# Delta-rule heads of a hybrid block: SiLU, gate exponentials, corner copies and norm roots set behind the next weights' high part, and both heads' transposes ahead of their copies

## The chip, the cores and the metric

One core of a Trainium2 chip runs the whole program in one launch. The metric is device microseconds (us) of an execution, and the median of several executions counts. The profile is of one such execution.

## The reference, cut to what matters

One encoder layer on 256 tokens with width 2048, all in float32:

```
h    = rms_norm(x, norm_mix_w) * (1 + scale_m) + shift_m
proj = h @ w_in                      # q,k,v,o of the mLSTM; q|k|v, z, beta, decay of the delta rule; two merge gates
qkv  = silu(centred_depthwise_conv(b_qkv, gdn_conv_w))          # 16 heads of 128
q_b  = l2_normalize(q) * B_DK ** -0.5;  k_b = l2_normalize(k)
o_b  = gated_delta_chunkwise(...) forward + backward            # needs the inverse of a unit triangular matrix
o_b  = rms_norm(o_b, gdn_norm_w);  y_b = (o_b * silu(b_z)) @ w_branch_b
h_a  = mLSTM forward + backward;   y_a = (sigmoid(a_o) * rms_norm(h_a)) @ w_branch_a
x    = x + gate_m * ((g_a * y_a + g_b * y_b) @ w_out)
x    = x + gate_f * (silu(gt) * up) @ w_down;   out = rms_norm(x)
```

The shifts, scales and gates come from `silu(c) @ ada_w + ada_b`, a 2048 by 12288 matrix that VectorE multiplies and sums row block by row block (`ada`, L110).

## The kernel before, in words

**Weights in two parts.** Every large projection is computed with each float32 weight split in two: `wh` is the weight rounded to the fast matmul format (a copy on ScalarE), `wl` is the rest (a subtraction on VectorE), and TensorE adds three products: high by high, high by low, low by high. A job loads 1 MB (`raw`, on SyncE's queue, three buffers) and cuts it into two halves. For each half ScalarE writes `wh`, VectorE writes `wl` (three buffers each), and TensorE then runs the half. `fjob` (L132, wh at L141, wl at L142) makes 128 features by 256 tokens, and its halves are named by 0 and 8; `tjob` (L153, wh at L166, wl at L167) makes 512 features for both token halves, with halves 0 and 2 of each of four chunks. So in the order `wh_z_0_2` is the second half of the first chunk of the z projection.

**The delta rule between the weights.** The first projection (L493) makes the gates and the q, k, v of heads 0 to 3. Then come 16 heads in four groups of four. For each head: `gdn_conv` copies a projection into a padded tile (`pad`, L279), applies the five taps (one on ScalarE L281, four on VectorE L283) and SiLU (L284) to give `kq` or `vf`. `gdn_phase1` builds the decays from scans (`dec`, L526 to L529), squares q and k (L534), transposes v and sums the squares on TensorE (`vps`, L537 and L539), takes a root (L546), forms k by k and k by q (`ks`, L565), multiplies by the decays on VectorE (L570 to L580), sends the diagonal blocks out (`inst_d`, L586, on GpSimd's queue) and copies the block corners (`cc`, L594 and L597, six calls on ScalarE).

For each group `gdn_invert` inverts the 32 by 32 diagonal blocks on VectorE (`uu`: a memset at L612, then 30 pairs of L617 and L623). `gdn_blocks` reads the inverses back, mixes them and copies them into `X` (L651) and into the diagonal of `UL` (L656, eight copies a group, all on ScalarE). `gdn_phase2` works on a pair of heads: four small matmul steps `p` (L671, L680, L693, L705) that complete `UL`, the applications `pa` (L718), `pb` (L729), `pc` (L718) and `po` (L744), the norm of each head (`gdn_norm`: squares L765, a root L769, a scaling L774), the transposes `px` (L754) and the copies `obt` (L756), which are stored. Head e's transposes are followed by head e's copy, and then comes the next head. Both heads' transposes write one PSUM tile.

**Fills and streams.** The delta rule is a long chain of small steps, so halves of the large projections stand between them: `fill(n)` issues n halves of jobs waiting in a list (z, v, o, the mLSTM's q and k called `a`, the merge gates `ma` and `mb`), and `stream` issues those of the next heads' q, k, v (`b`). The counts at each step are written out by hand (`after`, `last`, `fill(4)` in `invert`, `drive(..., 3)`). The sums of `ada` are pumped in every second job or so. What stands between two fills is placed by the program's order, with a scheduler that moves some instructions on each engine unless `order(...)` keeps them. On its engine each instruction waits for all ahead of it.

**After the delta rule** the scratch memory is closed (`sx.close`), and SyncE loads the stored heads (`o`, L877) and the mLSTM's q and k, v, and output gates (`mkq` L886, `vt` L888, `sgo` L890), while the last a and ma halves run. Then come the mLSTM, the branch projections, the output projection and the feed-forward part, none of which the diff touches.

A function in ScalarE's table (SiLU, the exponential, the root, the sigmoid) needs the table loaded: the profile shows `ACT_TABLE_LOAD` at the line of the function that follows.

Of the kernel before, what the change touches and what calls it, by code (L numbers as in the profile page):

```python
# [12 lines left out]
ALU = mybir.AluOpType  # L13
# [39 lines left out]
def hybrid_block(ctx: ExitStack, tc: tile.TileContext, xr, nfr, crow, pk_d, cst_d, ada2, ada4, win0, winb, wint, wba, wbb, wo, wgu, wd, out, dbg=None):  # L53
# [61 lines left out]

    background = []
# [15 lines left out]
    def fjob(name, src, done):  # L132
# [5 lines left out]
        for k0 in range(0, KB, 8):  # L138
            wh = st.tile([P, 8, P], F32R, tag="wh", bufs=3, name=f"wh_{name}_{k0}")
            wl = st.tile([P, 8, P], F32R, tag="wl", bufs=3, name=f"wl_{name}_{k0}")  # L140
            S.activation(wh, raw[:, k0 : k0 + 8], AF.Copy)  # L141
            V.tensor_tensor(wl, raw[:, k0 : k0 + 8], wh.bitcast(F32), ALU.subtract)  # L142
            for k in range(8):
                kk = k0 + k
                PE.matmul(o, wh[:, k], hh[:, kk], start=kk == 0, stop=False)  # L145
                PE.matmul(o, wh[:, k], hl[:, kk], start=False, stop=False)  # L146
                PE.matmul(o, wl[:, k], hh[:, kk], start=False, stop=kk == KB - 1)  # L147
            if k0:
                pump()
                done(o)  # L150
            yield True

    def tjob(name, chunks, xh, xl, done, early=0, by_token=False, steps=1):  # L153
# [6 lines left out]
        def halves(u, k0):  # L160
# [5 lines left out]
            order(S.activation(wh, raws[u][:, k0 : k0 + 2], AF.Copy), early)  # L166
            order(V.tensor_tensor(wl, raws[u][:, k0 : k0 + 2], wh.bitcast(F32), ALU.subtract), early)  # L167
# [96 lines left out]
    def gdn_conv(h, j, ps):  # L264
# [19 lines left out]
        S.activation(kq[:, j] if j < 2 else vf, cv, AF.Silu)  # L284
        if ps is None:
            evict(3 * h + j + 1 + NP_)
# [54 lines left out]
    def gates(w0, zz, first):  # L341
# [38 lines left out]
        S.activation(s2[32:64], sp[32:64], AF.Exp)  # L380
        G.dma_start(alpha_d.rearrange("d h t -> (d h) t"), s2[32:64])
# [16 lines left out]
        S.activation(ex[R], ex[R], AF.Exp)  # L398
        for v in range(2):
            r0 = 64 + 4 * v  # L400
            G.dma_start(mal_d[v], ex[r0 : r0 + 4, v, 0])
# [117 lines left out]
    def gdn_phase1(h):  # L519
        if h < GRP:  # L520
# [21 lines left out]
        yield  # L542
        sm = bk.tile([P, 12], F32, tag="sm", bufs=NB + 1, name=f"sm{h}")
# [48 lines left out]
        for b in range(4):  # L592
            r0, c0 = 32 * b, 32 * (b ^ 1)
            S.activation(cc[r0 : r0 + 32, 0, :, c0 : c0 + 32], (mb if b % 2 else mi)[r0 : r0 + 32, 0:2, c0 : c0 + 32], AF.Copy)  # L594
        for b in range(2):
            r0, c0 = 64 * b, 64 * (b ^ 1)
            S.activation(cc[r0 : r0 + 64, 1, :, c0 : c0 + 64], (mb if b else mi)[r0 : r0 + 64, 0:2, c0 : c0 + 64], AF.Copy)  # L597
# [34 lines left out]
    def gdn_blocks(g):  # L632
# [20 lines left out]
        for i, a in enumerate((F_, B_)):  # L653
            for b in range(4):
                r = slice(32 * b, 32 * b + 32)
                order(S.activation(UL[r, i, :, r], a[r], AF.Copy))  # L656
            yield

    def gdn_phase2(g, p):
# [90 lines left out]
        yield  # L750
        for e, on in enumerate(ons):
            h, hl_ = 4 * g + 2 * p + e, 2 * p + e
            for t in range(2):
                PE.transpose(px[:, (2 * e + t) * P : (2 * e + t + 1) * P], on[:, t], ident)  # L754
            obt = bk.tile([P, T], F32, tag="obt", bufs=2, name=f"obt{h}")
# [4 lines left out]
    def gdn_norm(g, h, hl_, po, r4):  # L760
# [8 lines left out]
        S.activation(so[:, 2:4], so[:, 2:4], AF.Sqrt, bias=epsc, scale=1.0 / (DK_B * DK_B))  # L769
        V.reciprocal(so[:, 2:4], so[:, 2:4])  # L770
        V.scalar_tensor_tensor(so[:, 4:6], rq, DK_B**-0.5, so[:, 2:4], ALU.mult, ALU.mult)
        sz = szs[g]
        for t in range(2):
            V.scalar_tensor_tensor(  # L774
                on[:, t], po[:, t * P : (t + 1) * P], so[:, 4 + t : 5 + t], sz[:, t, hl_ * P : (hl_ + 1) * P], ALU.mult, ALU.mult
            )
# [55 lines left out]
    def invert(g):  # L832
        gen = gdn_invert(g)
        next(gen)
        fill(4)
# [4 lines left out]
    for g in range(4):  # L840
# [503 lines left out]
```

## Time and profile before

| what | value |
|---|---|
| median of 3 executions | 2101.28 us (2100.79 to 2106.48) |
| the profiled execution | 2101.75 us |
| its span, first to last instruction | 2100.0 us |
| mean granted TensorE clock | 0.990 |
| TensorE (PE) busy | 2030.5 us, 97% |
| VectorE (DVE) busy | 1397.2 us, 67% |
| ScalarE (ACT) busy | 1056.9 us, 50% |
| GpSimd (POOL) busy | 95.8 us, 5% |

Stages by time from the span's start: first projection 0 to 147 us; gates 147 to 190; the first four heads to 260; the delta rule's groups with their fills to 975; the last fills, the mLSTM and the branch projections to 1250; output projection and norm to 1375; the feed-forward part to 2100.

A row of the timeline gives start, duration, engine, line, operation, output and inputs, and in brackets how long the engine was idle ahead of it and what ended that. The row of a stretch (windows) gives for each engine the busy time and, in parentheses, the number of instructions, then the granted clock as a share of full speed (PEclk), the share of time in which the DMA engines were busy, and GB/s. A group's row ends in its total busy time and the mean of one in ns, then the idle time ahead of it. Queues that issue DMAs are named by a q (SPq is SyncE's).

### The profile page before, as it was taken

Reading aid. Unit: us, or ns where it says so; the run is one execution under the profiler, and the core shown is the slowest. Engines: PE = TensorE matmul, PEld = TensorE weight load, DVE = VectorE, ACT = ScalarE, POOL = GpSimd, SP = SyncE. Lnnn points to the kernel's source line nnn. Section 1 sums busy time; section 2 is a strip of 40 time slices with the busy share of each in tenths; the row PEclk is TensorE's granted clock in tenths of the full one; section 3 lists DMA queues with packets and bytes.
Section 4 is the critical chain, followed back from the end, with each engine's and each line's share of the span. In section 5 each row is a group of like instructions: output and inputs, shape, how many; then the busy total and the mean of one; then the engine's idle time right before and its main releaser. Section 6 shows DMA issues by size and latency. Waiting matters only on the chain.

```text
span 2100.0 us, 27019 instructions
## 1 busy us (share of the span) xinstructions
PE 2030.5 (97%) x10374; PEld 1698.0 (81%) x10374; DVE 1397.2 (67%) x2060; ACT 1056.9 (50%) x1583; POOL 95.8 (5%) x189
## 2 busy tenths in 40 slices
PE   8999999999999999999999999799999999999998
PEld 6777789978988898888777877678888888878886
DVE  6787777777877687754677778665565554455554
ACT  3147548756774666565444443554444444444443
POOL 0002210110111011100000000000000000000000
PEclk9999999999999999999999999999999999999999
DMA  9986664566766565667886778466666665555553
GB/s 401 420 315 190 170 222 154 167 195 236 235 192 208 193 215 212 233 248 264 306 298 229 259 282 311 169 215 238 229 247 233 222 256 183 195 191 194 199 185 137
DMA packets 82035, 485.65 MB, mean 231 GB/s; under 512 B 10585, under 2 KB 20065, under 8 KB 27505
## 3 DMA queue, kind: packets, MB, share of 16 engines
q1 hardware_dynamic: 68736, 459.34, 60.4%
q0 software_dynamic: 5856, 9.49, 3.0%
q10 hardware_dynamic: 7314, 15.10, 1.9%
q8 instruction: 81, 1.33, 0.3%
q14 instruction: 48, 0.39, 0.1%
HBM read 467.07 MB, written 16.82 MB: 230 GB/s over the span
## 4 chain that ended last, share of the span: by engine, by line
PE 70%; DVE 6%; ACT 5%; DMA 5%; issue 2%; SPq 0%; ACTq 0%; DVEq 0%
PE acc_up L188 4%; PE acc_up L189 4%; PE acc_up L190 4%; PE acc_d L188 4%; PE acc_d L190 4%; PE acc_d L189 4%; PE acc_gt L189 4%; PE acc_gt L190 4%; PE acc_gt L188 4%; PE acc_b L147 2%; PE acc_b L145 2%; PE acc_b L146 2%; DMA ada<-ada 2%; PE acc_o L190 2%; PE acc_o L188 2%
## 5 line engine op out<-in xcount | busy, mean ns | idle before, releaser
L167 DVE TENSOR_TENSOR wl_d<-raw_d,wh_d 128x1024 fp32r<-128x1024 f32 x88 | 107.8, 1226 | 119.8 <-ACT wh_d L166 119.8
L167 DVE TENSOR_TENSOR wl_up<-raw_up,wh_up 128x1024 fp32r<-128x1024 f32 x88 | 107.7, 1225 | 110.0 <-ACT wh_up L166 110.0
L167 DVE TENSOR_TENSOR wl_gt<-raw_gt,wh_gt 128x1024 fp32r<-128x1024 f32 x88 | 107.9, 1226 | 100.0 <-ACT wh_gt L166 100.0
L145 PE MATMUL acc_b<-hh,wh_b 128*128 128x256 f32 x576 | 164.0, 285 | 4.2 <-ACT wh_b L141 4.2
L110 DVE SCALAR_TENSOR_TENSOR ada<-ada,crow 128x2048 f32<-128x2048 f32 x64 | 146.4, 2288 | 29.4 <-DMA ada<-ada 29.0
L147 PE MATMUL acc_b<-hh,wl_b 128*128 128x256 f32 x576 | 161.3, 280 | 1.4 <-DVE wl_b L142 1.4
L166 ACT ACTIVATE wh_d<-raw_d 128x1024 fp32r<-128x1024 f32 x88 | 93.3, 1060 | 137.4 <-PE acc_d L189 132.3
L146 PE MATMUL acc_b<-hl,wh_b 128*128 128x256 f32 x576 | 160.3, 279 | 0.0
L166 ACT ACTIVATE wh_gt<-raw_gt 128x1024 fp32r<-128x1024 f32 x88 | 93.3, 1060 | 127.0 <-PE acc_gt L189 77.2
L166 ACT ACTIVATE wh_up<-raw_up 128x1024 fp32r<-128x1024 f32 x88 | 93.2, 1060 | 117.4 <-PE acc_up L189 84.1
L189 PE MATMUL acc_gt<-wh_gt,hfl 128*128 128x512 f32 x352 | 139.1, 395 | 2.4 <-DVE hfl L1160 2.4
L188 PE MATMUL acc_gt<-wh_gt,hfh 128*128 128x512 f32 x352 | 137.9, 395 | 0.0
L190 PE MATMUL acc_gt<-wl_gt,hfh 128*128 128x512 f32 x352 | 137.7, 391 | 0.0
L188 PE MATMUL acc_up<-wh_up,hfh 128*128 128x512 f32 x352 | 137.1, 389 | 0.5 <-ACT wh_up L166 0.5
L189 PE MATMUL acc_up<-wh_up,hfl 128*128 128x512 f32 x352 | 137.0, 389 | 0.0
L190 PE MATMUL acc_up<-wl_up,hfh 128*128 128x512 f32 x352 | 136.9, 389 | 0.0
L188 PE MATMUL acc_d<-wh_d,ffh 128*128 128x512 f32 x344 | 134.4, 391 | 0.0
L189 PE MATMUL acc_d<-wh_d,ffl 128*128 128x512 f32 x344 | 134.4, 391 | 0.0
L190 PE MATMUL acc_d<-wl_d,ffh 128*128 128x512 f32 x344 | 133.9, 389 | 0.0
L493 PE MATMUL first<-x,raw 128*128 128x256 f32 x512 | 114.5, 382 | 7.8 <-ACT x L487 7.2
L493 PEld LDWEIGHTS first<-x,raw 128*128 128x128 f32 x512 | 96.1, 190 | 26.3 <-ACT x L487 13.8
L145 PEld LDWEIGHTS acc_b<-hh,wh_b 128*128 128x128 f32 x576 | 108.9, 189 | 4.6 <-ACT wh_b L141 4.5
(365 smaller groups left out, 5272.9 us busy)
## 6 DMA issues: line engine op xcount, KB each, us to landing
ada<-ada SPq DMA_DIRECT2D x64, 1024.0 KB, 5.1
raw_gt<-wgu SPq DMA_DIRECT2D x44, 1024.0 KB, 5.0
raw_up<-wgu SPq DMA_DIRECT2D x44, 1024.0 KB, 4.9
raw_d<-wd SPq DMA_DIRECT2D x44, 1024.0 KB, 4.8
raw_b<-winb SPq DMA_DIRECT2D x36, 1024.0 KB, 5.1
ra<-ada SPq DMA_DIRECT2D x32, 1025.0 KB, 15.6
raw<-win SPq DMA_DIRECT2D x16, 1024.0 KB, 14.6
raw_z<-wint SPq DMA_DIRECT2D x16, 1024.0 KB, 5.3
```

Of the source, the lines that this page charges most:

```text
L110: V.scalar_tensor_tensor(raw, raw, 1.0, row_c[:, :D], ALU.mult, ALU.mult, accum_out=mod[:, c0 + b : c0 + b + 1])
L145: PE.matmul(o, wh[:, k], hh[:, kk], start=kk == 0, stop=False)
L146: PE.matmul(o, wh[:, k], hl[:, kk], start=False, stop=False)
L147: PE.matmul(o, wl[:, k], hh[:, kk], start=False, stop=kk == KB - 1)
L166: order(S.activation(wh, raws[u][:, k0 : k0 + 2], AF.Copy), early)
L167: order(V.tensor_tensor(wl, raws[u][:, k0 : k0 + 2], wh.bitcast(F32), ALU.subtract), early)
L188: PE.matmul(ps[t], xh[:, kk, c], wh[:, k], start=kk == 0, stop=False)
L189: PE.matmul(ps[t], xl[:, kk, c], wh[:, k], start=False, stop=False)
L190: PE.matmul(ps[t], xh[:, kk, c], wl[:, k], start=False, stop=kk == last)
L493: PE.matmul(first[o], raw[:, o], x[:, b], start=b == 0 and o % 2 == 0, stop=b == KB - 1 and o % 2 == 1)
```

## The change

A list `behind` holds pieces of work that have been written but not yet issued, and `settle()` issues them. It is called in both kinds of jobs right behind `wh` and ahead of `wl`, at the start of `gdn_phase1`, ahead of its root, ahead of `px`, in the next `gdn_conv` (which leaves one piece in the list) and at the end. Into the list go: SiLU of each convolution; the two exponentials of the gates with the DMAs that store them; the corner copies of each head; and, in `gdn_norm`, the root with the scaling behind it. All but the DMAs and the VectorE part of the scaling are then kept in program order.

Three more edits: four of the eight copies of a group into the diagonal of `UL` (those with i = 1) go to VectorE; `px` of both heads is issued ahead of both `obt`; and the first group's inversion starts with six halves instead of four.

```
+    behind = []
+    def settle(keep=0):
+        while len(behind) > keep:
+            behind.pop(0)()
...
             S.activation(wh, raw[:, k0 : k0 + 8], AF.Copy)
+            settle()
             V.tensor_tensor(wl, raw[:, k0 : k0 + 8], wh.bitcast(F32), ALU.subtract)
...
             order(S.activation(wh, raws[u][:, k0 : k0 + 2], AF.Copy), early)
+            settle()
...
+        settle(1)
         cv = fr.tile([P, T], F32, tag="cv", bufs=2, name=f"cv{h}_{j}")
...
-        S.activation(kq[:, j] if j < 2 else vf, cv, AF.Silu)
-        if ps is None:
-            evict(3 * h + j + 1 + NP_)
+        def end():
+            order(S.activation(kq[:, j] if j < 2 else vf, cv, AF.Silu))
+            if ps is None:
+                evict(3 * h + j + 1 + NP_)
+        behind.append(end)
...
-        S.activation(s2[32:64], sp[32:64], AF.Exp)
-        G.dma_start(alpha_d.rearrange("d h t -> (d h) t"), s2[32:64])
+        def factors():
+            order(S.activation(s2[32:64], sp[32:64], AF.Exp))
+            G.dma_start(alpha_d.rearrange("d h t -> (d h) t"), s2[32:64])
+        behind.append(factors)
...
     def gdn_phase1(h):
+        settle()
...
         yield
+        settle()
         sm = bk.tile([P, 12], F32, tag="sm", bufs=NB + 1, name=f"sm{h}")
...
-            S.activation(cc[r0 : r0 + 32, 0, :, c0 : c0 + 32], (mb if b % 2 else mi)[r0 : r0 + 32, 0:2, c0 : c0 + 32], AF.Copy)
...
+        def corners():
+            for b in range(4):
+                r0, c0 = 32 * b, 32 * (b ^ 1)
+                order(S.activation(cc[r0 : r0 + 32, 0, :, c0 : c0 + 32], (mb if b % 2 else mi)[r0 : r0 + 32, 0:2, c0 : c0 + 32], AF.Copy))
...
+        behind.append(corners)
...
-                order(S.activation(UL[r, i, :, r], a[r], AF.Copy))
+                if i:
+                    order(V.tensor_copy(UL[r, i, :, r], a[r]))
+                else:
+                    order(S.activation(UL[r, i, :, r], a[r], AF.Copy))
...
         yield
+        settle()
         for e, on in enumerate(ons):
             h, hl_ = 4 * g + 2 * p + e, 2 * p + e
             for t in range(2):
                 PE.transpose(px[:, (2 * e + t) * P : (2 * e + t + 1) * P], on[:, t], ident)
+        for e in range(2):
+            h, hl_ = 4 * g + 2 * p + e, 2 * p + e
             obt = bk.tile([P, T], F32, tag="obt", bufs=2, name=f"obt{h}")
             S.activation(obt, px[:, e * T : (e + 1) * T], AF.Copy, scale=pk[:, PK_GNW + h : PK_GNW + h + 1])
...
-        S.activation(so[:, 2:4], so[:, 2:4], AF.Sqrt, bias=epsc, scale=1.0 / (DK_B * DK_B))
...
+        def scaled():
+            order(S.activation(so[:, 2:4], so[:, 2:4], AF.Sqrt, bias=epsc, scale=1.0 / (DK_B * DK_B)))
+            V.reciprocal(so[:, 2:4], so[:, 2:4])
+            V.scalar_tensor_tensor(so[:, 4:6], rq, DK_B**-0.5, so[:, 2:4], ALU.mult, ALU.mult)
...
+        behind.append(scaled)
...
     def invert(g):
         gen = gdn_invert(g)
         next(gen)
-        fill(4)
+        fill(4 if g else 6)
```

In the whole program ScalarE has 60 table loads instead of 70, and 16 copies fewer; VectorE has 16 more. TensorE's instructions are the same in number.

**ScalarE at the end of the second group's second pair** (620 us in the trace; `so` are the norm roots, `nn` the root of the last head's squares, `cc` its corners, `ev` evictions of a projection, `obt` the copies of `px`). Before:

```order
L296 ACTIVATE ev_o_5396<-acc_o_1_4022 128x512
L546 ACT_TABLE_LOAD
L546 ACTIVATE nn_5480<-vps_5407,epsc 128x4
L556 ACTIVATE vv_5486<-vps_5407,nn_5480 128x128
L594 ACTIVATE cc_1107<-mi_5489 32x2x32 x2
L594 ACTIVATE cc_1107<-mb_5490 32x2x32 x2
L597 ACTIVATE cc_1107<-mi_5489 64x2x64
L597 ACTIVATE cc_1107<-mb_5490 64x2x64
L756 ACTIVATE obt_5521<-px_1_5327,pk 128x256
L166 ACTIVATE wh_z_0_0_5534<-raw_z_0_5532 128x1024
L757 DMA ob_d_115<-obt_5521 128x256
L756 ACTIVATE obt_5526<-px_1_5327,pk 128x256
```

And now:

```order
L806 ACT_TABLE_LOAD
L806 ACTIVATE so_5378<-so_5378,epsc 128x2
L806 ACTIVATE so_5384<-so_5384,epsc 128x2
L148 ACTIVATE wh_a_1_8_5510<-raw_a_1_5480 128x1024
L174 ACTIVATE wh_z_0_0_5596<-raw_z_0_5594 128x1024
L317 ACTIVATE ev_a_0_5462<-acc_a_0_5389 128x256
L570 ACTIVATE nn_5542<-vps_5472,epsc 128x4
L174 ACTIVATE wh_z_0_2_5612<-raw_z_0_5594 128x1024
L174 ACTIVATE wh_z_1_0_5630<-raw_z_1_5628 128x1024
L790 ACTIVATE obt_5585<-px_1_5364,pk 128x256
L790 ACTIVATE obt_5588<-px_1_5364,pk 128x256
L620 ACTIVATE cc_1107<-mi_5551 32x2x32
```

The two roots share a table load with each other and with `nn`; three halves' `wh` stand ahead of the copies, and the corners behind them. The weights of z no longer stand behind a copy that waits for a transpose.

**VectorE at the first inversion** (252 to 262 us; `uu` is the inverse in work, `dec` a decay scan of a later head). Before:

```order
L167 TENSOR_TENSOR wl_v_0_2_1700<-raw_v_0_1681,wh_v_0_2_1699 128x1024
L527 SCALAR_TENSOR_TENSOR dec_2471<-al_2215,cst 128x128
L528 SCALAR_TENSOR_TENSOR dec_2471<-al_2215,cst 128x256
L529 SCALAR_TENSOR_TENSOR dec_2471<-al_2215,cst 128x128
L167 TENSOR_TENSOR wl_v_1_0_1727<-raw_v_1_1724,wh_v_1_0_1726 128x1024
L612 MEMSET uu_1234 64x32
L617 TENSOR_TENSOR utmp_1640<-uu_1234 64x30
```

And now:

```order
L176 TENSOR_TENSOR wl_v_0_2_1700<-raw_v_0_1681,wh_v_0_2_1699 128x1024
L552 SCALAR_TENSOR_TENSOR dec_2505<-al_2249,cst 128x128
L176 TENSOR_TENSOR wl_v_1_0_1718<-raw_v_1_1715,wh_v_1_0_1717 128x1024
L176 TENSOR_TENSOR wl_v_1_2_1734<-raw_v_1_1715,wh_v_1_2_1733 128x1024
L640 MEMSET uu_1234 64x32
L645 TENSOR_TENSOR utmp_1640<-uu_1234 64x30
```

The memset stands one low part later.

**SyncE at the end of the delta rule** (975 to 995 us; the merge gate's chunks `raw_ma` around the loads of the mLSTM). Before:

```order
L163 DMA raw_ma_0_9095<-wint 128x2048
L877 DMA o_0_8885<-ob_d_114 128x4x256
L877 DMA o_1_8887<-ob_d_115 128x4x256
L886 DMA mkq_8951<-kq_d_94 128x4x256
L888 DMA vt_8953<-v_d_98 128x1024
L890 DMA sgo_8955<-o_d_102 128x1024
L886 DMA mkq_8960<-kq_d_95 128x4x256
L888 DMA vt_8962<-v_d_99 128x1024
L890 DMA sgo_8964<-o_d_103 128x1024
L877 DMA o_2_9131<-ob_d_116 128x4x256
L163 DMA raw_ma_1_9133<-wint 128x2048
L163 DMA raw_ma_2_9199<-wint 128x2048
```

And now:

```order
L171 DMA raw_ma_0_9092<-wint 128x2048
L171 DMA raw_ma_1_9126<-wint 128x2048
L916 DMA o_0_8944<-ob_d_114 128x4x256
L916 DMA o_1_8946<-ob_d_115 128x4x256
L925 DMA mkq_9010<-kq_d_94 128x4x256
L927 DMA vt_9012<-v_d_98 128x1024
L929 DMA sgo_9014<-o_d_102 128x1024
L925 DMA mkq_9019<-kq_d_95 128x4x256
L927 DMA vt_9021<-v_d_99 128x1024
L929 DMA sgo_9023<-o_d_103 128x1024
L171 DMA raw_ma_2_9164<-wint 128x2048
L916 DMA o_2_9162<-ob_d_116 128x4x256
```

With two halves more issued at the first inversion, all later fills stand two halves earlier: one chunk more is loaded ahead of the block of loads, and `raw_ma_2` stands ahead of `o_2`.

More of the change, by code (lines that the diff above doesn't have):

```diff
@@ L397, in gates, with weights @@
             yield
[L398 to L401, printed above, removed]
+        def weights():
+            order(S.activation(ex[R], ex[R], AF.Exp))
+            for v in range(2):
+                r0 = 64 + 4 * v
+                G.dma_start(mal_d[v], ex[r0 : r0 + 4, v, 0])
+        behind.append(weights)
         gdn_conv(1, 0, None)
@@ L591, in gdn_phase1 @@
         cc = ccs[h % NB]
-        for b in range(4):
-            r0, c0 = 32 * b, 32 * (b ^ 1)
-            S.activation(cc[r0 : r0 + 32, 0, :, c0 : c0 + 32], (mb if b % 2 else mi)[r0 : r0 + 32, 0:2, c0 : c0 + 32], AF.Copy)
-        for b in range(2):
-            r0, c0 = 64 * b, 64 * (b ^ 1)
-            S.activation(cc[r0 : r0 + 64, 1, :, c0 : c0 + 64], (mb if b else mi)[r0 : r0 + 64, 0:2, c0 : c0 + 64], AF.Copy)
+        def corners():
+            for b in range(4):
+                r0, c0 = 32 * b, 32 * (b ^ 1)
+                order(S.activation(cc[r0 : r0 + 32, 0, :, c0 : c0 + 32], (mb if b % 2 else mi)[r0 : r0 + 32, 0:2, c0 : c0 + 32], AF.Copy))
+            for b in range(2):
+                r0, c0 = 64 * b, 64 * (b ^ 1)
+                order(S.activation(cc[r0 : r0 + 64, 1, :, c0 : c0 + 64], (mb if b else mi)[r0 : r0 + 64, 0:2, c0 : c0 + 64], AF.Copy))
+        behind.append(corners)
         heads[h] = (cc, gg, at, vv, r4, sg3)
@@ L768, in gdn_norm @@
         V.tensor_tensor(so[:, 2:4], so[:, 2:4], so[:, 0:2], ALU.mult)
-        S.activation(so[:, 2:4], so[:, 2:4], AF.Sqrt, bias=epsc, scale=1.0 / (DK_B * DK_B))
-        V.reciprocal(so[:, 2:4], so[:, 2:4])
-        V.scalar_tensor_tensor(so[:, 4:6], rq, DK_B**-0.5, so[:, 2:4], ALU.mult, ALU.mult)
         sz = szs[g]
[L773 to L776, printed above, removed]
+        def scaled():
+            order(S.activation(so[:, 2:4], so[:, 2:4], AF.Sqrt, bias=epsc, scale=1.0 / (DK_B * DK_B)))
+            V.reciprocal(so[:, 2:4], so[:, 2:4])
+            V.scalar_tensor_tensor(so[:, 4:6], rq, DK_B**-0.5, so[:, 2:4], ALU.mult, ALU.mult)
+            for t in range(2):
+                V.scalar_tensor_tensor(
+                    on[:, t], po[:, t * P : (t + 1) * P], so[:, 4 + t : 5 + t], sz[:, t, hl_ * P : (hl_ + 1) * P], ALU.mult, ALU.mult
+                )
+        behind.append(scaled)
         return on
@@ L865, in hybrid_block @@
             invert(g + 1)
+    settle()
     sx.close()
```

## The prediction

> **What bounds the kernel now.** I read the page first, then the stages in windows, then each of TensorE's waits in the timeline, and last the granted clock around them.
>
> ```profile
> PE 2030.5 (97%) x10374; PEld 1698.0 (81%) x10374; DVE 1397.2 (67%) x2060; ACT 1056.9 (50%) x1583; POOL 95.8 (5%) x189
> PE 70%; DVE 6%; ACT 5%; DMA 5%; issue 2%; SPq 0%; ACTq 0%; DVEq 0%
> ```
>
> TensorE bounds it: busy 97% of the span and 70% of the chain that ended last. The change takes nothing from TensorE's work, so it can only win the time in which TensorE stands still, and the time in which it runs at a lower clock. The windows show where that is, in the stages that the diff touches:
>
> ```profile
> 147.00:190.00 43.00, 37.97 (x167) 29.54 (x165) 36.07 (x64) 29.62 (x41) 7.27 (x14) 1.00 0.67 202
> 190.00:260.00 70.00, 66.94 (x280) 52.00 (x280) 48.21 (x116) 41.40 (x77) 16.20 (x30) 0.95 0.61 179
> 480.00:617.00 137.00, 135.67 (x991) 124.16 (x990) 108.13 (x203) 102.64 (x198) 14.27 (x28) 1.00 0.70 234
> 617.00:720.00 103.00, 92.39 (x550) 81.97 (x551) 72.52 (x130) 56.28 (x89) 9.92 (x19) 0.95 0.55 186
> 975.00:1000.00 25.00, 24.96 (x179) 23.02 (x178) 9.53 (x8) 9.21 (x12) 2.17 (x4) 1.00 0.93 317
> ```
>
> The second number less the third is TensorE's idle time: 5.0 us in the gates, 3.1 and 10.6 at 190 and 617, but only 1.3 in the long stretch from 480. So the delta rule is mostly covered already, and the loss sits in a few places. These are TensorE's waits there, in order of time; the bracket has the idle time and what ended it:
>
> ```profile
> 161.25 0.51 PE L188 MATMUL acc_z<-wh_z,hh 128*128 128x512 f32 x1 [1.51 <-ACT wh_z L166]
> 163.63 0.74 PE L190 MATMUL acc_z<-wl_z,hh 128*128 128x512 f32 x2 [0.46 <-DVE wl_z L167]
> 172.65 0.50 PE L190 MATMUL acc_v<-wl_v,hh 128*128 128x512 f32 x1 [1.64 <-DVE wl_v L167]
> 220.12 0.44 PE L537 MATMUL vps<-cst,vf 128*128 128x128 f32 x2 [1.02 <-ACT vf L284]
> 221.70 0.80 PE L190 MATMUL acc_v<-wl_v,hh 128*128 128x512 f32 x1 [1.14 <-DVE wl_v L167]
> 260.88 0.50 PE L190 MATMUL acc_v<-wl_v,hh 128*128 128x512 f32 x1 [1.77 <-DVE wl_v L167]
> 515.62 0.38 PE L718 MATMUL pa<-vv,UL 128*128 128x128 f32 x1 [1.12 <-ACT UL L656]
> 620.89 0.69 PE L754 MATMUL px<-cst,on 128*128 128x128 f32 x2 [3.95 <-ACT obt L756]
> 621.84 0.79 PE L188 MATMUL acc_z<-wh_z,hh 128*128 128x512 f32 x1 [0.26 <-ACT wh_z L166]
> 702.42 0.42 PE L145 MATMUL acc_b<-hh,wh_b 128*128 128x256 f32 x1 [1.94 <-ACT wh_b L141]
> 716.99 0.38 PE L145 MATMUL acc_b<-hh,wh_b 128*128 128x256 f32 x1 [2.26 <-ACT wh_b L141]
> 718.25 0.38 PE L147 MATMUL acc_b<-hh,wl_b 128*128 128x256 f32 x1 [0.76 <-DVE wl_b L142]
> 1003.82 0.80 PE L188 MATMUL acc_ma<-wh_ma,hh 128*128 128x512 f32 x1 [3.83 <-ACT wh_ma L166]
> ```
>
> Most are ended by a weight part that ScalarE or VectorE made late. The granted clock shows a second price:
>
> ```profile
> 221.30:228.13 6.83, 6.43 (x19) 5.46 (x20) 3.72 (x12) 3.20 (x8) 0.56 (x1) 0.50 0.79 133
> 262.30:265.71 3.41, 3.41 (x9) 2.69 (x9) 3.24 (x8) 1.06 (x1) 0.00 (x0) 0.50 0.65 269
> 620.70:627.53 6.83, 6.38 (x15) 4.74 (x16) 4.63 (x6) 3.94 (x6) 3.02 (x7) 0.50 0.66 95
> 702.60:706.01 3.41, 3.41 (x17) 3.41 (x18) 1.45 (x2) 2.77 (x6) 0.00 (x0) 0.50 0.35 98
> 1003.00:1009.83 6.83, 6.01 (x14) 4.75 (x15) 6.03 (x10) 4.52 (x5) 0.42 (x1) 0.50 0.62 219
> ```
>
> Each stretch has half the clock. The work done in it would have taken half its busy time, so the drops cost 6.43/2 = 3.2, 1.7, 3.2, 1.7 and 3.0 us. Their starts lie on a grid: 41.0, 358.4, 81.9 and 300.4 us apart are 12, 105, 24 and 88 times 3.413. And in the cell of 3.41 us ahead of each start TensorE was idle for 1.02 + 0.74, 1.77, 3.75, 1.94 and 3.0 us, while the wait of 1.64 us ahead of 172.65 lies inside one cell (170.1 to 173.5 on this grid) and was followed by none, and that of 2.26 us ahead of 716.99 is cut at 716.25 into 1.52 and 0.74. So as I read it a cell that is idle for more than about 1.7 us, half of it, halves the next one or two. A wait under 1.7 us costs itself; a longer one costs 1.7 to 3.2 us more, if its place in the cell is bad.
>
> [...]
>
> **The change part by part.**
>
> *Gates (147 to 190).* What ScalarE does ahead of the late high part at 161 us:
>
> ```profile
> 157.30 0.42 ACT L284 ACTIVATE kq<-cv 128x256 f32<-128x256 f32 x1 [3.96 <-DVE cv L283]
> 158.41 1.28 ACT L380 ACT_TABLE_LOAD   x1
> 160.14 1.06 ACT L166 ACTIVATE wh_z<-raw_z 128x1024 fp32r<-128x1024 f32 x1
> ```
>
> ScalarE waits 3.96 us for taps, then does SiLU, a table load and the exponential, and only then `wh`. In the new order that `wh` stands behind the padding copy and ahead of the next taps and the exponential: the waits of 1.51 and 0.46 go (1.97). Behind the exponential are queued its own store, the decay loads and their scans, which now stand behind a low part that they stood ahead of; for the 1.64 I take half, 0.8. Ends: 0 and 5.0, the stage's whole idle time. Taken: 2.8.
>
> *First inversion (260).*
>
> ```profile
> 258.76 0.20 DVE L617 TENSOR_TENSOR utmp<-uu 64x30 f32<-64x30 f32 x1 [5.28 <-issue]
> ```
> ```profile
> 261.38 0.23 PE acc_v L188
> ```
>
> The first row is VectorE's: it stands 5.28 us at the memset of `uu` until the blocks have come back by DMA, and the low parts behind it stand too. The second, of the chain, is one of TensorE's steps there at the full clock. The new order has one more low part ahead of the memset, which is one half more of TensorE's work, 12 such steps or 2.75 us; that covers the 1.77 us with 1.0 to spare, and the drop of 1.7 goes with it. Taken: 3.5. Ends: 0 and 3.5.
>
> *Diagonal of UL (515).* Four copies leave ScalarE's queue ahead of `pa` and join VectorE's, between taps:
>
> ```profile
> L656 ACT ACTIVATE UL<-cg 32x256 f32<-32x256 f32 x32 | 13.2, 412 | 0.3
> L707 DVE COPY UL<-p 64x256 f32<-64x256 f32 x8 | 3.4, 428 | 1.7 <-ACT UL L706 1.5
> ```
>
> No row shows these copies on VectorE; the nearest, its copy at L707, has 428 ns against ScalarE's 412, and reads PSUM, not SBUF. Four would take 1.7 us on either engine, so `pa` waits about as long as before: I take 0.4 gained, between 1.12 and a loss of 1.7 in each of four groups.
>
> *Transposes and roots (620).* ScalarE's copy that released the second head's transposes started here:
>
> ```profile
> 619.72 0.31 ACT L597 ACTIVATE cc<-mi 64x128 f32<-64x128 f32 x1
> 620.37 0.47 ACT L756 ACTIVATE obt<-px,pk 128x256 f32<-128x256 f32 x1
> L769 ACT ACT_TABLE_LOAD x14 | 18.0, 1283 | 0.2
> ```
>
> The copy is the second row. It stood behind the last root of `vps` and the corners, which waited for VectorE, and z's first `wh` stood behind it. Now the second head's transposes don't need it, and `wh_z_0_0` stands ahead of the last root: 3.95 + 0.26 and the drop of 3.2 go. Next late is `on`, whose root stands ahead of `wh_a_1_8` with one table load for both heads (1.28 us by the third row, where there were two), a whole half of TensorE earlier. Taken: 7.4. Ends: 3.0 and 7.4. What stands behind the copies now is the corners, needed only in the next group.
>
> *Streams (700 and 715).*
>
> ```profile
> 714.64 0.42 ACT L284 ACTIVATE kq<-cv 128x256 f32<-128x256 f32 x1 [3.91 <-DVE cv L283]
> ```
>
> At 715 ScalarE stands 3.91 us in front of a SiLU with `wh_b` behind it. That is what the list takes away: of 2.26 + 0.76 I take 2.5. The 1.94 at 702 is a `wh_b` behind the copies of L656 in a row, after a weight that came late; half of the copies stay, so I take half of 1.94 + 1.7, 1.8. Taken: 4.3. Ends: 0 and 6.7.
>
> *Fills two halves earlier (1003).*
>
> ```profile
> 991.74 0.37 SPq L877 DMA_DIRECT2D o<-ob_d  x1
> 992.97 2.17 SPq L163 DMA_DIRECT2D raw_ma<-wint  x3
> 1002.71 1.06 ACT L166 ACTIVATE wh_ma<-raw_ma 128x1024 fp32r<-128x1024 f32 x1 [11.24 <-DMA raw_ma<-wint]
> ```
>
> `raw_ma_1` was issued at 992.97 behind the block of loads and landed 9.7 us later. In the new order it stands ahead of the block, and `raw_ma_2`, the next one behind it, stands ahead of `o_2`: issued 1.2 us sooner, with half a megabyte less in front (1.6 us at the 317 GB/s of the window from 975). But the fills left behind the block are the same in number, so the wait doesn't go: it shrinks from 3.83 to about 1.0, under half a cell, and the drop of 3.0 may go. Between 0 and 6.8 I take 4.0. The loads of `o` now stand behind a `raw` that waits for a buffer, which delays the mLSTM's first loads by at most a half or two; those loads have TensorE's eight halves behind them.
>
> *What is left alone:* the waits ended by `vf` and `wl_v` at 220 (VectorE has the same work there in both orders), those of `wl` between the steps of the later inversions, and all behind 1090.
>
> *Sum.* 2.8 + 3.5 + 0.4 + 7.4 + 4.3 + 4.0 = 22.4 us. Against it stands what the new order will expose: SiLU, roots and corners of 16 heads come a `wh` later, VectorE has 16 copies more, and every weight load moves. The trace has no row for that. From below it is nothing; from above all the 22.4. I take two new waits of the size of that at 260.88 with its drop, 3.5 each: 7.0. That leaves 15.4 us. The profiled execution took 2101.75 us (2100.0 and 1.75 around it) and the median is 2101.28, so the numbers hold for both: 2101.3 - 15.4 = 2086 us.
>
> **The rivals.**
>
> *More than I take.* Nothing new is exposed, and the drop at 221 goes as well, since its cell was idle by only 1.76 us and the grid will lie otherwise: 22.4 + 3.2 = 25.6, so 2076 us. For it: most of the waits ended by weights are of the same kind, and the list acts on all of them. Against: ScalarE and VectorE work in order, and something is always last.
>
> *Given back at pa.* The diagonal's copies on VectorE stand behind taps and a low part, in stretches where VectorE is busy 108.13 of 137 us. If `pa` of each group waits 1.7 us longer and each time loses 1.7 us of clock, that is 4 x 3.4 = 13.6 on top of the 7.0: 1.8 us are left, 2099.5 us, no change. For it: `pa` is already late by 1.12 us at 515. Against: ScalarE has 1.7 us less there and makes the other four sooner.
>
> *Slower: SiLU and roots come late.* This row shows what they would stand behind:
>
> ```profile
> L141 ACT ACTIVATE wh_b<-raw_b 128x1024 fp32r<-128x1024 f32 x72 | 75.3, 1057 | 42.2 <-PE acc_b L146 23.8 <-DMA raw_b<-winb 12.0 <-PE acc_o L189 4.4
> ```
>
> A `wh` takes 1.06 us and often waits, for a weight to land or a buffer that TensorE still reads; a SiLU behind it waits too, and with it `vps`, as a root does with `px`. That is 16 + 8 places at 1.06 + 0.41 = 1.5 us. It decides when over half of them are bare: 12 x 1.5 = 18, with half of those losing about 2.4 us of clock, 14: 32 - 22.4 = 10 us slower, 2111 us. For it: `vps` waited for `vf` at 220. Against: of 16 heads only that one did, and a half of TensorE's work usually lies between.
>
> **How the numbers follow.** My forecast has 0.51, the larger gain 0.20, the gain given back 0.19, slower 0.10. A measurement of this kernel can tell about 0.3%, 6.3 us, from no change: faster is under 2095, and both first cases lie there, 0.71; same 0.19; slower 0.10. The range goes from 2072, a little past the larger gain, to 2101, past the one given back: some 0.05 lies below it and 0.15 above.
>
> **What would show it.** In the new profile the rows of `px` and `acc_z` at 620 should have no wait of over 1 us and no slice at half clock; the stage at 617 should have under 5 us of idle TensorE in 100; the wait on `wl_v` at 260 should be gone; the one on `wh_ma` near 990 should be under 2 us. The drops should be two or three instead of five up to 1010. I am wrong if `vps`, `px` or `pa` show new waits of over 1.5 us in several groups, or if the waits on `wh` and `wl` in the streams are still there, ended by the same lines at other times.

## The result, and the profile after

| kernel | median, us | lowest to highest | executions |
|---|---|---|---|
| before | 2101.34 | 2097.92 to 2107.58 | 8 |
| changed | 2086.05 | 2078.75 to 2095.21 | 8 |

The changed kernel takes 0.9927 of the time of before, 95% interval 0.9909 to 0.9946: 15.3 us faster. The forecast was 2086. As the experiments show, the total came out right, but several of its terms were credited to the wrong edit. Two single executions further down (one of the kernel before, 2542 us, and one with five halves, 5111 us) were in a far slower state and are left out of the ratios and of the medians given here.

The profiled execution is the slowest of the eight: 2095.21 us, of which the span is 2093.4. It is 6.5 us shorter than the profiled one of before, and not 15; what it shows is a place, not the whole gain. In windows of the stages (TensorE's busy time is the second number, the granted clock the third from the end):

```profile
147.00:190.00 43.00, 38.88 (x174) 30.63 (x173) 38.56 (x72) 30.07 (x43) 8.65 (x15) 1.00 0.68 205
190.00:260.00 70.00, 68.60 (x299) 53.18 (x298) 53.94 (x128) 46.71 (x83) 14.90 (x29) 1.00 0.64 192
480.00:617.00 137.00, 135.09 (x1015) 125.40 (x1014) 112.94 (x219) 96.93 (x199) 13.04 (x26) 1.00 0.71 236
617.00:720.00 103.00, 100.81 (x648) 90.14 (x647) 80.58 (x148) 60.45 (x93) 9.66 (x19) 1.00 0.59 199
720.00:960.00 240.00, 231.81 (x1389) 202.33 (x1389) 168.43 (x307) 139.62 (x253) 18.07 (x34) 0.98 0.65 221
```

From 190 to 260 TensorE is now idle 1.4 us (3.1 before) and from 617 to 720 2.2 us (10.6 before), both at the full clock. The gates won only 0.9 us. In the last row 8.2 us are idle (2.1 in the longer stretch of before), and the clock fell too, to a mean of 0.98 (1.00 in that stretch of before). The waits behind these numbers, from TensorE's timeline:

```profile
175.06 0.50 PE L199 MATMUL acc_v<-wl_v,hh 128*128 128x512 f32 x1 [0.74 <-DVE wl_v L176]
179.59 0.50 PE L199 MATMUL acc_v<-wl_v,hh 128*128 128x512 f32 x1 [1.50 <-DVE wl_v L176]
...
219.43 0.44 PE L560 MATMUL vps<-cst,vf 128*128 128x128 f32 x2 [1.09 <-ACT vf L296]
...
514.71 0.49 PE L749 MATMUL pa<-vv,UL 128*128 128x128 f32 x2 [0.67 <-DVE UL L685]
...
747.85 1.46 PE L711 MATMUL p<-R,pt 128*128 128x32 f32 x6 [3.29 <-DVE pt L703]
...
903.62 0.68 PE L760 MATMUL pb<-z,gg 128*128 128x128 f32 x4 [2.29 <-DVE r L761]
...
997.33 0.80 PE L197 MATMUL acc_ma<-wh_ma,hh 128*128 128x512 f32 x1 [4.94 <-ACT wh_ma L174]
```

Gone are the waits at 161, 260, 620, 702, 717 and that on `wl_v` at 221. New are two in the gates, one of 3.29 us on a step `p` of the third group and one of 2.29 in the last group, both ended by VectorE. The wait on `wh_ma` is longer than before. And the clock, in windows laid on its drops (the last number but two):

```profile
747.72:754.55 6.83, 6.70 (x31) 6.73 (x32) 4.13 (x5) 2.03 (x5) 2.42 (x5) 0.50 0.56 186
904.74:908.15 3.41, 3.41 (x14) 3.01 (x13) 1.43 (x2) 2.20 (x5) 0.00 (x0) 0.50 0.71 271
996.89:1000.30 3.41, 2.97 (x7) 2.42 (x8) 2.99 (x3) 2.43 (x4) 0.00 (x0) 0.50 0.64 257
1020.79:1024.20 3.41, 3.41 (x8) 2.32 (x7) 3.41 (x4) 1.28 (x2) 0.00 (x0) 0.50 0.57 148
```

The four drops of before up to 703 are gone; three follow the three long waits, and the fourth follows no wait at all (last section). In us, the two new places cost 3.29 + 3.35 and 2.29 + 1.7, 10.6 together, where I had allowed 7.0 for what the new order would expose. Of the five signs that the prediction named, four came: no long wait and no drop at 620, 2.2 us of idle time at 617, no wait at 260, and three drops up to 1010. The fifth, a wait on `wh_ma` of under 2 us, did not. None of the five tells which edit did it, and so each edit was run by itself.

### The profile page after: what moved, and what is told of

The parts are those of the page before. It is cut to its first block, busy times and chain, and to the rows that moved or that the text cites. A ratio compares the mean times of both kernels' runs of the same rounds, so it can differ in the third digit from the quotient of the medians.

```text
span 2093.4 us, 27008 instructions
## 1 busy us (share of the span) xinstructions
PE 2029.6 (97%) x10374; PEld 1698.2 (81%) x10374; DVE 1399.4 (67%) x2076; ACT 1037.9 (50%) x1557; POOL 96.2 (5%) x189
## 4 chain that ended last, share of the span: by engine, by line
PE 72%; DVE 11%; DMA 9%; ACT 5%; issue 2%; POOL 0%; ACTq 0%; SPq 0%; DVEq 0%; POOLq 0%
PE acc_up L197 4%; PE acc_up L198 4%; PE acc_up L199 4%; PE acc_d L199 4%; PE acc_d L197 4%; PE acc_d L198 4%; PE acc_gt L198 4%; PE acc_gt L199 4%; PE acc_gt L197 4%; DMA ra<-ada 3%; PE acc_o L199 2%; PE acc_o L197 2%; PE acc_o L198 2%; DMA ada<-ada 2%; PE acc_b L153 2%
## 5 line engine op out<-in xcount | busy, mean ns | idle before, releaser
L155 PEld LDWEIGHTS acc_b<-hh,wl_b 128*128 128x128 f32 x576 | 109.4, 190 | 0.9 <-DVE wl_b L150 0.9
```

## The experiments

Theory of places: the gain is the sum of single waits, and each edit takes away the one that its part of the prediction names. Rival, a shifted order: two more halves at the first inversion move every later half of the fills against the delta rule's steps, and this renews all the waits behind it. All ratios are to the kernel before, run on the same chip as the kernel in question; 0.001 is 2.1 us, and the gains in us are worked out from the ratios.

### Each edit on its own

Six halves at the first inversion, alone:

```
-        fill(4)
+        fill(4 if g else 6)
```

> The kernel before with one edit: the first inversion starts with six halves instead of four. Theory of places (the gain of 15 us is a sum of single waits, each edit removing its own): the wait on wl_v at 260 (1.8 us) and its clock drop (1.7) go and little else, 3.5 us faster, about 2098. Rival, a shifted order (all later fills stand two halves earlier, so that any shift renews all later waits): the waits at 515, 617, 702 and 717 go or change by more than 1 us each, and the time moves by more than 8 us either way.

Measured: 2089.86 us, 0.9947 (0.9926 to 0.9967). The line that I had worth 3.5 us at its own place, and a few more at 1003, gives 11 by itself (12.5 by the medians, the figure that later expectations use). Between 610 and 720 its profile has one wait of over 0.7 us (1.2 on `wl_a`, which the others have too) where before had 3.95, 1.94 and 2.26, although neither the list nor the new order of the transposes is in it.

Both heads' transposes ahead of both copies, alone:

```
                 PE.transpose(px[:, ...], on[:, t], ident)
+        for e in range(2):
+            h, hl_ = 4 * g + 2 * p + e, 2 * p + e
             obt = bk.tile([P, T], F32, tag="obt", bufs=2, name=f"obt{h}")
```

> The kernel before with one edit: both heads' transposes ahead of both copies. Places: the wait of 3.95 us on px at 617 and its drop go, 7 us faster, about 2094, all else as before. Rival: without the list the roots, table loads and corners still stand ahead of z's first high part on ScalarE, so that wh_z at 620 is late instead and TensorE waits 2 to 4 us there all the same, at most 2 us faster.

Measured: 2103.12 us, 1.0005 (0.9987 to 1.0022), nothing. Its profile shows the rival, with more than the 2 to 4 us expected: the wait at 617 changes its name and grows.

```profile
621.66 0.79 PE L188 MATMUL acc_z<-wh_z,hh 128*128 128x512 f32 x1 [5.68 <-ACT wh_z L166]
```

The transposes no longer wait, and TensorE waits for the next high part, which stands behind the same roots and table loads on ScalarE.

The list alone (the changed kernel with the other three edits taken back):

```
-                if i:
-                    order(V.tensor_copy(UL[r, i, :, r], a[r]))
-                else:
-                    order(S.activation(UL[r, i, :, r], a[r], AF.Copy))
+                order(S.activation(UL[r, i, :, r], a[r], AF.Copy))
...
-        for e in range(2):
-            h, hl_ = 4 * g + 2 * p + e, 2 * p + e
             obt = ...
...
-        fill(4 if g else 6)
+        fill(4)
```

> The changed kernel without its three smaller edits: the list alone (SiLU, exponentials, corners and roots behind the next high part), with UL all on ScalarE, copies between the transposes and four halves at the first inversion. Places: gains in the gates (1), at 219 (4) and at 700 to 717 (6), less what the new order exposes at 744 and 901 (about 7), so 4 to 8 us faster, about 2095; px at 617 may lose its wait too, since ScalarE no longer has the root and the corners ahead of the copy, which would add 5. Rival: the list does nearly all of it, 13 us or more, and the other edits are worth nothing.

Measured: 2097.82 us, 0.9977 (0.9958 to 0.9996), 4.8 us faster. TensorE's waits in its timeline:

```profile
256.88 0.50 PE L199 MATMUL acc_v<-wl_v,hh 128*128 128x512 f32 x1 [2.73 <-DVE wl_v L176]
...
614.84 0.73 PE L199 MATMUL acc_z<-wl_z,hh 128*128 128x512 f32 x2 [1.82 <-DVE wl_z L176]
...
694.07 0.39 PE L153 MATMUL acc_b<-hh,wh_b 128*128 128x256 f32 x1 [2.13 <-ACT wh_b L148]
708.74 0.44 PE L153 MATMUL acc_b<-hh,wh_b 128*128 128x256 f32 x1 [2.50 <-ACT wh_b L148]
```

At 617 the list does what I thought the transposes would do. In the streams the two waits on `wh_b` are as long as before (2.13 and 2.50 for 1.94 and 2.26), and ScalarE's timeline shows why for the second:

```profile
706.39 0.42 ACT L296 ACTIVATE kq<-cv 128x256 f32<-128x256 f32 x1 [3.91 <-DVE cv L293]
...
707.64 1.05 ACT L148 ACTIVATE wh_b<-raw_b 128x1024 fp32r<-128x1024 f32 x1
```

The SiLU that I had put the wait down to still stands ahead of `wh_b`, with the same 3.91 us behind the taps. One high part goes ahead of it (at 700.01), but one did before too (at 708.25 there), and the late one follows it in both. So the list does not reorder this place, and the run doesn't tell what a SiLU behind the late `wh_b` would have been worth.

The changed kernel with four halves:

```
-        fill(4 if g else 6)
+        fill(4)
```

> The changed kernel with four halves again at the first inversion. Places: the wait at 260 comes back, 1.8 us and in some executions its drop of 1.7, so 2 to 4 us slower than the change, about 2089. Rival, a shifted order: more than 6 us from the change either way, with other waits at 744, 901 and 992.

Measured: 2100.92 us, 0.9996 (0.9981 to 1.0010). Without that line the whole change is worth nothing. The waits in its timeline:

```profile
255.71 0.50 PE L199 MATMUL acc_v<-wl_v,hh 128*128 128x512 f32 x1 [2.26 <-DVE wl_v L176]
...
511.03 0.80 PE L749 MATMUL pa<-vv,UL 128*128 128x128 f32 x2 [2.84 <-DVE UL L685]
...
693.72 0.39 PE L153 MATMUL acc_b<-hh,wh_b 128*128 128x256 f32 x1 [2.70 <-ACT wh_b L148]
708.20 0.56 PE L153 MATMUL acc_b<-hh,wh_b 128*128 128x256 f32 x1 [2.57 <-ACT wh_b L148]
```

The streams' waits are back. And `pa` waits 2.84 us for the copies that went to VectorE, where before had 1.12 and the list alone has 1.12 too, and a drop of 6.8 us starts there (at 510.29, TensorE busy for 6.09 of it; a matmul of `acc_b` took 0.41 us at 512.69 and 0.28 at 507.91): my rival "given back at pa", at one place. That is 1.7 + 3.0 us more than in the list alone, which is 4 us faster in all. The longest wait of this profile is another, 3.57 us at 816 on `wh_z`.

### Place or shift

Six halves and then six instead of eight in the first group, so that nothing behind is shifted; and four, then ten, which shifts without touching the first inversion:

```
-        fill(4)
+        fill(4 if g else 6)
...
-        fill(8)
+        fill(8 if g else 6)
```

> The kernel before with six halves at the first inversion and two fewer (6 instead of 8) right behind it in the first group, so that only the place at 260 changes and all later fills stand where they were. If the 12 us of six halves alone come from that place: 10 us or more faster, about 2090. If they come from the shift of all later halves (theory now): 2 to 4 us faster, about 2099, with the waits at 617, 700 and 715 back.

```
-        fill(8)
+        fill(8 if g else 10)
```

> The kernel before with four halves at the first inversion and two more (10 instead of 8) right behind it: the shift without the place at 260. Shift: 8 to 10 us faster, about 2093, with the wait of 1.8 us at 260 kept and those at 617, 700 and 715 gone. Place: at most 2 us either way.

Measured: 2098.26 us, 0.9985 (0.9976 to 0.9995), for the place alone; 2093.85 us, 0.9967 (0.9954 to 0.9980), for the shift alone. That is 3.2 and 6.9 us, together 10.1, against 11.1 for both in one. The place is worth about what the forecast said, and the shift twice that. The first kernel's waits:

```profile
617.18 0.69 PE L754 MATMUL px<-cst,on 128*128 128x128 f32 x2 [3.96 <-ACT obt L756]
...
700.63 0.38 PE L145 MATMUL acc_b<-hh,wh_b 128*128 128x256 f32 x1 [2.77 <-ACT wh_b L141]
715.20 0.53 PE L145 MATMUL acc_b<-hh,wh_b 128*128 128x256 f32 x1 [2.50 <-ACT wh_b L141]
```

And the second's, which has the wait at 260, while those at 617, 700 and 715 are gone:

```profile
258.94 0.50 PE L190 MATMUL acc_v<-wl_v,hh 128*128 128x512 f32 x1 [1.67 <-DVE wl_v L167]
```

What a shift of two halves does at 617 is seen on ScalarE. Before:

```profile
609.13 1.28 ACT L296 ACT_TABLE_LOAD   x1
610.42 0.60 ACT L296 ACTIVATE ev_o<-acc_o 128x512 f32<-128x512 f32 x1
611.04 1.28 ACT L769 ACT_TABLE_LOAD   x1
612.33 0.29 ACT L769 ACTIVATE so<-so,epsc 128x2 f32<-128x2 f32 x1
612.65 1.28 ACT L296 ACT_TABLE_LOAD   x1
613.94 0.60 ACT L296 ACTIVATE ev_o<-acc_o 128x512 f32<-128x512 f32 x1
614.56 1.28 ACT L546 ACT_TABLE_LOAD   x1
```

With six halves alone, at the same step:

```profile
609.98 1.28 ACT L769 ACT_TABLE_LOAD   x1
611.27 0.30 ACT L769 ACTIVATE so<-so,epsc 128x2 f32<-128x2 f32 x1
611.59 1.28 ACT L284 ACT_TABLE_LOAD   x1
...
613.71 1.06 ACT L141 ACTIVATE wh_a<-raw_a 128x1024 fp32r<-128x1024 f32 x1
614.78 1.28 ACT L769 ACT_TABLE_LOAD   x1
```

Before, the o job ended just here. Its two evictions go through the sigmoid, and they fell between the norm's root and the next root: four table loads in a row, 5.1 us, with no weight between them. In all, ScalarE makes no high part for 14.3 us there (from 606.44 to `wh_z` at 620.74 in the prediction's stretch). Two halves earlier the job's end lies elsewhere, and the longest such stretch between 605 and 618 is 6.1 us, up to the `wh_a` at 613.71.

Is it that the fills start earlier, or only where the ends of jobs fall? Two more sizes of the shift:

```
+        fill(4 if g else 8)
```

> The kernel before with eight halves at the first inversion, a shift of four. If an earlier start of the fills helps as such (more work done ahead, weights loaded sooner): as fast as six or faster, 2090 or below. If it matters only where the ends of the jobs, with their evictions, table loads and ada sums, fall against the steps of the delta rule: anything from 2088 to 2105, with waits at other places than with six, and the place at 260 covered in either case.

```
+        fill(4 if g else 5)
```

> The kernel before with five halves at the first inversion, a shift of one. Earlier start: about half of what six give, 2095. Where the ends fall: again anything from 2088 to 2105; the ends of jobs move by one half, so I expect the waits at 617 and 715 to be smaller but not gone. The place at 260 has no half more between the low part of v_1_0 and the memset than it needs, about 1 us less wait.

Measured: eight, 2099.59 us, 0.9996 (0.9983 to 1.0008); five, 2093.22 us, 0.9966 (0.9952 to 0.9980), its executions from 2086 to 2101. So 4, 5, 6 and 8 halves give 0, 7, 11 and 1 us. An earlier start as such would have made eight at least as good as six. With eight the waits at 260 and 617 are gone, and others stand elsewhere: 2.17 us at 725 on `wh_b`, 1.75 at 944, and the longest one here, ahead of eight matmuls that took 1.89 us (0.97 for the eight at 689.49 in the kernel before):

```profile
567.37 1.89 PE L671 MATMUL p<-R,cc 128*128 128x32 f32 x8 [2.84 <-DVE at L575]
```

With five, the waits at 617 and 715 are gone where I had expected smaller ones, and the one at 260 is 1.35 us, 0.4 less and not 1. So it is where things fall that counts. Which alignment is a good one can't be told from four counts, and no run moved the end of a single job by itself.

### On top of six halves

The list and six halves, with UL all on ScalarE and each head's copy between the transposes:

```
-                if i:
-                    order(V.tensor_copy(UL[r, i, :, r], a[r]))
-                else:
-                    order(S.activation(UL[r, i, :, r], a[r], AF.Copy))
+                order(S.activation(UL[r, i, :, r], a[r], AF.Copy))
...
-        for e in range(2):
-            h, hl_ = 4 * g + 2 * p + e, 2 * p + e
             obt = ...
```

> The change without two of its edits: the list and six halves, but UL all on ScalarE and each head's copy between the transposes. If the parts add (six alone 12.5 us, list alone 4.6), 2084 or below. If the list only treats places that the shift had already freed, the same as six alone, 2089 to 2090. If the other two edits carry something beside them, slower than the change.

The change with only the first of these two edits taken back:

> The change with the eight copies into UL all on ScalarE again. My forecast's term was 0.4 us, so within 2 us of the change. Rival, given back at pa: the copies on VectorE make pa late in each group, and without them it is 3 to 6 us faster than the change.

The changed kernel again, beside them:

> The changed kernel once more, beside the others on the same chip: 2086 within 3 us. If the waits at 744 and 901 come from the order, this profile has them again; if they come from when a DMA happened to land, it has others of their kind.

| kernel | median, us | lowest to highest | ratio (95%) |
|---|---|---|---|
| list and six | 2079.02 | 2075.91 to 2081.67 | 0.9889 (0.9870 to 0.9909) |
| change, UL on ScalarE | 2079.62 | 2076.33 to 2084.76 | 0.9894 (0.9874 to 0.9914) |
| change again | 2087.05 | 2079.12 to 2093.84 | 0.9928 (0.9903 to 0.9954) |

The list and six halves alone beat the change by 8 us, and before by 23. The order of the transposes is worth nothing on top (0.0005, inside the intervals). The copies of UL on VectorE cost about 7 us; with six executions each the two intervals still touch, but the first eight executions of the change lie as high (median 2086.05). With six halves they also widen the scatter (lowest to highest 14.7 and 16.5 us, against 5.8 and 8.4 without them). On top of six halves the list seems worth more than by itself: 0.9947 to 0.9889 is 12 us, for 4.8 alone. The two were measured in different sets of runs, and the excess over a plain sum, about 7 us, is about what the intervals of the three kernels together allow by chance. That the parts do not add is likely, then, and not shown.

The change again has the wait at 744, of another size, and a longer one at a step where its first profile had 0.81 (at 934):

```profile
749.45 1.05 PE L711 MATMUL p<-R,pt 128*128 128x32 f32 x8 [2.15 <-DVE pt L703]
...
930.78 1.10 PE L736 MATMUL p<-X,pt 128*128 128x64 f32 x8 [1.62 <-DVE pt L725]
```

The same steps with UL on ScalarE:

```profile
747.52 1.05 PE L708 MATMUL p<-R,pt 128*128 128x32 f32 x8 [0.92 <-DVE pt L700]
...
927.15 1.10 PE L733 MATMUL p<-X,pt 128*128 128x64 f32 x8 [1.03 <-DVE pt L722]
```

So the wait at 744 belongs to the order (3.29 and 2.15 us in two executions, and 2.44 in the kernel of the next section, which is the same up to there), and is smaller without the copies on VectorE; the one at 901 was 0.70 the second time, and in the first profile VectorE stood 2.5 us there until a row block of `ada` had landed. These two rows differ by 1.8 us, and 7 were measured. A drop of 3.41 us, worth 1.7, follows the step at 930 and the one at 927 alike (the two matmuls of `wl_o` behind them took 1.01 and 1.20 us, where two of `acc_o` in a row, from 930.63 in the changed kernel's first profile, took 0.62). The rest isn't tied to a place: a copy takes 283 ns on VectorE (16 of them, 4.5 us) and 412 on ScalarE, so its own length is not the cause. Whether it was the order in which VectorE's other work follows was not tried.

### The wait that stayed

The second mLSTM head's loads behind `raw_ma_2` instead of ahead of it:

```
-    cores = steps(mlstm(0), mlstm(1))
+    first, second = mlstm(0), mlstm(1)
+    cores = steps(first, second)
...
-    fill(2)
-    next(cores)
-    fill(6)
+    fill(2)
+    next(first)
+    fill(6)
...
+    next(second)
+    fill(2)
     next(cores)
-    fill(5)
+    fill(3)
```

> The change with the second mLSTM head's loads (1.5 MB) behind raw_ma_2 instead of ahead of it. The wait on wh_ma near 992 is 4 to 5 us with a drop of 1.5 to 3 in every run so far, six halves or four. If the DMA engines are full there (over 390 GB/s from 985 on), 1.5 MB less in front of raw_ma_2 brings it about 3.8 us sooner, the wait falls to 1 us or less and the time by 4 to 6 us against the change. Rival: the engines are as full behind it, and raw_ma_3 or the loads themselves are late instead, no gain.

In the changed kernel, SyncE's issue of `raw_ma_2`, its use on ScalarE, and the window around them (DMA share and GB/s are the last two):

```profile
982.23 0.48 SPq L171 DMA_DIRECT2D raw_ma<-wint  x1
...
996.22 1.06 ACT L174 ACTIVATE wh_ma<-raw_ma 128x1024 fp32r<-128x1024 f32 x1 [11.55 <-DMA raw_ma<-wint]
```

```profile
985.00:995.00 10.00, 7.39 (x33) 5.81 (x31) 1.12 (x1) 0.00 (x0) 0.00 (x0) 1.00 1.05 401
```

With the loads spread:

```profile
984.92 0.50 PE L197 MATMUL acc_ma<-wh_ma,hh 128*128 128x512 f32 x1 [1.44 <-ACT wh_ma L174]
986.18 0.50 PE L199 MATMUL acc_ma<-wl_ma,hh 128*128 128x512 f32 x1 [0.53 <-DVE wl_ma L176]
...
987.70 0.50 SPq L171 DMA_DIRECT2D raw_ma<-wint  x1
...
996.16 0.80 PE L197 MATMUL acc_ma<-wh_ma,hh 128*128 128x512 f32 x1 [2.49 <-ACT wh_ma L174]
```

Measured: 2088.34 us, 0.9932 (0.9909 to 0.9956), no gain against 0.9928. The wait of 4.20 to 4.94 us has become three, 4.46 together: 1.44 on `raw_ma_2`, a little more than the 1 us expected, and then the next chunk is late instead. That is the rival. Why that chunk is late has two candidates. The DMA engines move 333 to 387 GB/s from 970 to 985 and 422 from 990 to 995, close to the 401 of the changed kernel. But from 985 to 990 they move only 256, and `raw_ma_3` is issued only at 987.70 (the SPq row), behind a load of `o` that had stood 6.6 us for its buffer. Whether the bytes or the place in the queue decide was not separated. The premise that every run had 4 to 5 us there was also too wide: 2.60 with six and then six halves, 2.54 with eight.

## Why the prediction was right, and where it wasn't

**The size of the whole.** 22.4 us less 7.0 was forecast, and 15.3 measured. The mechanism, waits and clock drops of TensorE in a handful of places, held: TensorE's idle time and half of its busy time at half the clock add up to 84.7 us in the profile before (69.5 + 15.2) and 62.6 in that of the list with six halves (54.8 + 7.8), 22.1 less for spans 22.7 us apart. But that the total hit 2086 was luck: most of the terms and the allowance were off in ways that happened to cancel.

**First inversion, 3.5.** Right: the place alone gave 3.2.

**Transposes and roots, 7.4.** The wait went, but not by the edit named. The transposes alone give nothing (5.68 on `wh_z` for 3.95 on `px`); the list alone leaves 1.82 of it; six halves alone remove all of it. The step that failed is the sentence that the wait is one of copies and corners ahead of z's high part. What the prediction names there, the last root with its table load and the corners with their wait for VectorE, is 1.6 + 3.2 us of the 14.3 in which ScalarE makes no high part. The end of the o job just ahead of it, two evictions and three more table loads, takes 5.4 (609.13 to 614.56); the trace of before shows it, and I did not price it. How much of the wait each of the two makes was not run apart. A slip beside it: the idle time of 3.75 us in the cell ahead of 620.7 can't be, since a cell has 3.41; TensorE was idle from 616.94 to 620.89, so all of the cell was.

**Streams, 4.3.** The waits went, but the step failed: the shift removes them, with or without the list, and the list alone leaves them (2.13 and 2.50). At 715 the list does not set that SiLU behind the late `wh_b`: it stood behind one high part and ahead of the next already, and still does. At 702 I counted half of the copies into `UL` as gone, but the four ahead of that `wh_b` are those with i = 0, which stay on ScalarE: with the copies divided and four halves the wait is 2.70.

**Fills two halves earlier, 4.0 at 1003.** The place was wrong, the size of the shift too small: 6.9 us alone, and hardly any of it at 1003, where that kernel still waits 4.58 us. I looked for the shift's effect only where a load was moved, and took the order between 260 and 975 as otherwise unchanged. The wait on `wh_ma` did not shrink: `raw_ma_2` was issued at 982.23, with the DMA engines at 401 GB/s from 985 on, and its first use came 14 us later.

**Diagonal of UL, 0.4.** Its sign was wrong: it costs about 7 us. The bound of 1.7 us lost in each of four groups comes near in size (6.8), but not as a mechanism: with six halves `pa` waits 0.67 us at 514, less than before, and no long wait on `UL` is in that profile. Only with four halves did `pa` pay. Where the 7 us are lost stays open.

**Gates, 2.8.** 0.9 measured in the windows. The wait on `wh_z` went, and two on `wl_v` came (0.74 and 1.50 for 1.64).

**Left alone, the waits at 220.** The one on `wl_v` and the drop behind it, 1.1 + 3.2 us, went in every kernel with the list, and stayed in every kernel without it. That order had moved there too, so this is a gain of the list that I had put at nothing.

**What the new order exposes, 7.0.** 10.6 at 744 and 901 in the first profile; in the second 2.15 and 0.70 with no drop, and 1.62 with a drop worth 1.7 at 930. The estimate had no row behind it, and the scatter of the executions is as large as it is.

## What to carry to other kernels

Where fills stand in a long in-order program, a change in one early count moves every later job's end, with its evictions and table loads, against the steps in between: four counts of one early fill gave 0, 7, 11 and 1 us here. Price the shift as an edit of its own, and try several counts by themselves before the structural edits, since they can be worth more than these. A list that sets work behind the next weight changes nothing where it stood there already, so read in the new order whether the piece really moved. And take a change of several edits apart before keeping it: here two of four carried everything, one did nothing and one cost about a third of what the rest had won.

## What the runs showed of the hardware

The prediction read the clock too simply. The drops of the changed kernel start on a grid as in the prediction, 157.02, 92.15 and 23.90 us apart, which is 46, 27 and 7 times 3.413; but one of them follows a cell without any idle time. Ahead of the drop at 1020.79 TensorE has no gap, but this:

```profile
1017.49 2.73 PE L969 MATMUL pden<-ones,mdec 128*128 128x1 f32 x24
```

Twenty-four matmuls with one column each filled 2.73 of the 3.41 us, and the granted clock in the next 3.41 was 0.50. In the list with six halves the same step (at 1002.26, 2.73 us) is followed by a drop at 1004.99. The step stands twice in the program. The second time in the changed kernel, at 1114.28, 2.08 us of it lie in one cell, and the clock was 1.00 in that cell and the next. In the kernel before it was 1.00 behind the second time too (at 1125.09, with 1.99 us in one cell), and no drop follows the first, at 1013.17, which ran in pieces of 1.84, 0.28 and 0.72 us with matmuls of 512 columns between them. In the kernel with six halves alone, the drop at 220.46 (the window below) follows a cell with only 1.2 us of idle time, in which most of the eight one-column matmuls of `vps` (0.95 us from 216.81) and parts of the two waits shown here lie:

```profile
220.46:227.29 6.83, 5.89 (x18) 5.02 (x19) 4.02 (x11) 3.48 (x8) 0.89 (x3) 0.50 0.67 107
```

```profile
219.82 0.44 PE L537 MATMUL vps<-cst,vf 128*128 128x128 f32 x2 [1.01 <-ACT vf L284]
221.40 1.22 PE L190 MATMUL acc_v<-wl_v,hh 128*128 128x512 f32 x2 [1.15 <-DVE wl_v L167]
```

Why the clock fell behind these steps was not shown: no run here varied the columns or the gaps by themselves. The "half a cell" of the prediction is no sharp bound either. In the kernel before, the cells from 1245.30 and 1248.71, idle for 1.85 and 1.96 us, were followed by no drop, while the one ahead of 262.30, idle for 1.77, was; and in the changed kernel the cell from 1304.09, idle for 1.68, was followed by 3.41 us at 0.50. The wait of 2.29 us ahead of 903.62 was followed by the drop at 904.74.

A copy of 32 by 256 float32 within SBUF took 283 ns on VectorE and 412 ns on ScalarE (16 of each in the changed kernel). The forecast had taken VectorE's copy of 64 by 256 out of PSUM, 428 ns, as its price.
